# The feed-forward's squared root moved behind the second product, and seven Strassen products on three shared accumulators

## The chip, the cores and the metric

The kernel runs on one core of a Trainium2 chip. The metric is the device time of one execution in microseconds (us): the median of several runs. The profile is a hardware trace of one execution; its span goes from the first instruction to the last.

## What is computed

The reference is a two-layer trunk on one sequence of 512 tokens with 1024 channels. Each layer has an attention part (eight stick-breaking heads and four differential heads) and a feed-forward part; a last RMS norm closes it. The change lies in the feed-forward part and in what follows it:

```python
def rmsnorm(x, g):
    y = xf * lax.rsqrt(jnp.mean(xf * xf, axis=-1, keepdims=True) + EPS) * g
...
    h = rmsnorm(x, mlp_norm[l])
    u = jnp.square(jax.nn.relu(jnp.einsum('bsd,df->bsf', h, w_ff1[l])))   # 1024 -> 4096
    x = x + jnp.einsum('bsf,fd->bsd', u, w_ff2[l])                        # 4096 -> 1024
return rmsnorm(x, final_norm)
```

With r = rsqrt(mean + EPS), one number for each token, the hidden values are relu(r * z)^2 = r^2 * relu(z)^2, since r is positive. So r may be applied before the square, or r^2 = 1 / (mean + EPS) after the second product, where the token lies on the partitions.

## The kernel before

Everything is fp32 carried as two fp32r halves (hi and lo), and each product of two such pairs is three matmuls (`three`, L273: hi by hi, hi by lo, lo by hi). Activations lie transposed, channels on partitions and tokens along the free axis, until the second product of the feed-forward; its result has tokens on partitions.

**One group of the feed-forward.** The 4096 hidden channels go in four groups (`GROUPS`). In a group, eight blocks (`block`, L286) each make 128 hidden channels by 512 tokens in one PSUM bank, 24 matmuls of 512 columns. `evict_u` (L862) takes a block out: relu times r (`rbc`, r spread over the partitions, L872, VectorE), the square (L873, ScalarE), and then the sums and differences of the Winograd form of Strassen's method (tile `F`, one buffer), split into hi and lo (`Ah`, `Al`). The second product is then done as seven products of half size, named in `FORMS`: 11, x3, x2, 22, x1, 21, x4. Each has 24 matmuls too, in two banks (token rows r = 0 and 1), the two rows in turn. `gather` (L891) adds a finished product to its running sum in SBUF, `y[form]`: a ScalarE copy the first time, afterwards a VectorE add (L898).

**Banks.** Of the eight PSUM banks two carry the tag `t` (transposes), two `mm`, three `s`, one `o`. Each of the seven products of the kernel before asks for a fresh pair, (s, s), (s, o) and (mm, mm) in turn, so a pair comes back after two other products.

**The seven sums** are turned into the four quadrants of the result only after the last group: `join` (VectorE, L904) and `merge` (an accumulating transfer from SBUF to SBUF issued by GpSimd, L907).

**The start of a feed-forward.** `rms_a` (L253) turns the squares' sum with four small PE transposes into one column for each row block and takes the power -0.5 on GpSimd. `rms_b` (L267) spreads it with four more transposes and a ScalarE copy into `rbc`. The first two blocks of the first group wait with their eviction until `rbc` is there.

**The ends.** After the first layer `back` (L924) turns the result's columns with four transposes each and adds them to x; four columns run beside the last product x4, the four others beside the first product of the next layer. In the last layer `forth` (L910) turns x into the sums at the start, and the last product x4 is done row 0 first, then row 1 in two column halves (`tail`). While it runs, VectorE and ScalarE finish the other rows: `square` (sum of squares), `root` (VectorE sum, L961, then a power on GpSimd, L963), `weigh` and `store`. `last_row` and `store_last` close the last row. The order of these steps on VectorE is written out in the list `first`, that on ScalarE in `squares`, and `in_order` fixes both.

**Order elsewhere.** A list scheduler places each engine's instructions; program order is its priority, so a step can be put ahead of one that it judges not ready. `behind` fixes single orders. Weight units are split into hi and lo (`split_part`, L110: ScalarE L123 by way of L108, VectorE L124) three units ahead of their use, and the operands of the seven forms grow in place by accumulating transfers (`fetch`, `grow`).

Of the kernel before, what the change touches and what calls it, by code (L numbers as in the profile page):

```python
# [17 lines left out]
P = 128  # L18
# [25 lines left out]
CAME = (4, 5, 6, 7, 0, 1, 2, 3)  # L44
# [117 lines left out]
def trunk(ctx, tc, opened, xT, w, w2, gfin, lamv, cos, sin, out):  # L162
# [62 lines left out]
    ms = cp.tile([P, 4], F32, tag="ms", name="ms")  # L225
    fin = cp.tile([P, 24], F32, tag="fin", name="fin")
    cp.tile([P, 40], F32, tag="trail", name="trail")
# [38 lines left out]

    def rms_b(bc, name, col, tag="t"):  # L267
        pt = bank(tag, "rb_" + name)
        for j in range(4):
            nc.tensor.transpose(pt[:, j * P : (j + 1) * P], col[:, j : j + 1].to_broadcast([P, P]), ident)  # L270
        nc.scalar.copy(bc, pt)

    def three(pt, a, b, first, last):  # L273
        ah, al = a
        bh, bl = b
        nc.tensor.matmul(pt, ah, bh, start=first, stop=False)  # L276
        nc.tensor.matmul(pt, ah, bl, start=False, stop=False)  # L277
        nc.tensor.matmul(pt, al, bh, start=False, stop=last)  # L278
# [33 lines left out]
    for l in range(L):  # L312
        with ExitStack() as actx:
# [52 lines left out]
            came = CAME if l else range(KC)  # L366
# [7 lines left out]
            squares = [add_sq(c, n == 0, tt, nc.vector) for n, c in enumerate(came)]  # L374
# [441 lines left out]
        with ExitStack() as fctx:  # L816
# [4 lines left out]
            y = {f: (fe if f in ("11", "x3") else fp).tile([P, 2, 512], F32, tag="y" + f, name=f"y{f}_{l}") for f in FORMS}  # L821
# [26 lines left out]
            for g in range(GROUPS):  # L848
                for c in range(GP // 2):
                    for form, fn, args in (  # L850
                            ("11", grow, (g, "x1", "12", c)), ("x3", grow, (g, "x2", "11", c)),
                            ("x2", grow, (g, "x4", "21", c)), ("22", grow, (g, "21", "21", c)),
                            ("x1", fetch, (g + 1, "11", c)), ("x4", fetch, (g + 1, "x3", c)),
                            ("21", fetch, (g + 1, "22", c))):
                        if g + 1 < GROUPS or fn is grow:
                            W.then.setdefault(unit(g, form, c), []).append(lambda fn=fn, args=args: fn(*args))
            for form in ("11", "x3", "22"):
                for c in range(GP // 2):
                    fetch(0, form, c)
            W.pools.append(f2)  # L860

            def evict_u(pt, g, k, forms):  # L862
# [9 lines left out]
                nc.vector.scalar_tensor_tensor(out=t, in0=pt, scalar=0.0, in1=rbc, op0=ALU.max, op1=ALU.mult)  # L872
# [12 lines left out]
            fresh = set(FORMS) - ({"21", "22", "x1", "x4"} if last else set())  # L885
            home = {(1, 0): "21", (1, 1): "22", (0, 0): "x4", (0, 1): "x1"}

            def place(tb, j):
                return y[home[(tb // 2, j)]][:, tb % 2, :]

            def gather(form, banks_, rs=(0, 1)):  # L891
                steps = []
                for r in rs:
                    o = y[form][:, r, :]
                    if form in fresh:
                        steps.append(nc.scalar.copy(o, banks_[r]))
                    else:
                        steps.append(nc.vector.tensor_add(o, o, banks_[r]))  # L898
                if 1 in rs:
                    fresh.discard(form)  # L900
                return steps

            def join(to, by):
                return nc.vector.tensor_add(y[to], y[to], y[by])  # L904

            def merge(to, by):
                nc.gpsimd.dma_start(  # L907
                    y[to].rearrange("p a t -> p (a t)"), y[by].rearrange("p a t -> p (a t)"), accum_op=ALU.add)

            def forth(tb, j):  # L910
# [3 lines left out]
                if j == 0:  # L914
                    nc.scalar.copy(place(tb, j), pt)
                elif tb < 2:
                    nc.scalar.activation(y["x1"][:, tb, :], pt, AF.Copy, scale=-1.0)
                else:
                    nc.vector.scalar_tensor_tensor(
                        out=place(tb, j), in0=pt, scalar=-1.0, in1=y["x1"][:, tb - 2, :], op0=ALU.mult, op1=ALU.subtract)  # L920
# [15 lines left out]
            def last_row(banks_):  # L936
                half = [place(1, 0)[:, 0:256], banks_[1][:, 0:256]]
                m = [fin[:, n : n + 1] for n in (8, 9, 10, 11, 0)]
                add = nc.vector.tensor_add(half[0], half[0], banks_[0][:, 0:256])
                ends = [nc.scalar.activation(  # L940
                    ft(f"junk1{n}")[:, 0:256], half[n], AF.Square, accum_out=m[0] if n == 0 else m[4]) for n in range(2)]
# [6 lines left out]
            def store_last(bank_):  # L948
                o, r = place(1, 0), fin[:, 11:12]
                done = store(1, 1, True)  # L950
                for n in range(2):
                    cols = slice(256 * n, 256 * n + 256)
                    nc.vector.scalar_tensor_tensor(
                        out=o[:, cols], in0=bank_[:, 0:256] if n else o[:, cols], scalar=r, in1=cos_t[:, cols],
                        op0=ALU.mult, op1=ALU.mult)
                    nc.sync.dma_start(out[1, :, cols], o[:, cols])
# [13 lines left out]
            def store(tb, j, weighed):  # L970
# [7 lines left out]
                (nc.scalar if (tb, j) == (1, 1) else nc.sync).dma_start(out[tb, :, 512 * j : 512 * j + 512], o)  # L978
# [16 lines left out]
            for g in range(GROUPS):  # L995
                forms = {}
                end = g == GROUPS - 1
                if g == 1:
# [9 lines left out]
                waiting = []  # L1008
                for k in range(2 * GP):
                    for n, pt in enumerate(block(f"f{l}_{g}_{k}", "any")):  # L1010
                        if (g, k, n) == (0, 1, 0):
                            rms_a(ssq, 1.0 / D, rcol, f"m{l}")
                        if (g, k, n) == (0, 2, 4):
                            rms_b(rbc, f"m{l}", rcol)
                    waiting.append((pt, k))
                    if g == 0 and k < 2:
                        continue
                    for one, i in waiting:
                        evict_u(one, g, i, forms)
                    waiting = []  # L1020
# [3 lines left out]
                for f, form in enumerate(FORMS):  # L1024
                    to = [bank((("s", "s"), ("s", "o"), ("mm", "mm"))[f % 3][r], f"{form}{l}{g}{r}") for r in range(2)]
                    work = [(c, i, r, 0) for c in range(GP // 2) for i in range(2) for r in range(2)]
                    tail = end and form == "x4"
                    if tail and last:
                        work = [(c, i, r, n) for r, n in ((0, 0), (1, 1), (1, 2)) for c in range(GP // 2) for i in range(2)]
# [3 lines left out]
                        seed = nc.scalar.copy(halves[1][:, 0:256], y["x4"][:, 1, 256:512])  # L1033
                    elif end and last and form == "21":
                        work.sort(key=lambda e: e[2])
                    held = {}
                    for n, (c, i, r, part) in enumerate(work):
# [10 lines left out]
                        three(pt, (hi[:, SIDE[form], rs], lo[:, SIDE[form], rs]), b_, n == mine[0] and part < 2, n == mine[-1])  # L1048
                        if tail and last and n == 3:
                            squares.append(square(2, 0))  # L1050
# [5 lines left out]
                        if end and not last and form == "x4" and n % 2:  # L1056
                            h = back(4 + n // 2)
# [4 lines left out]
                    came = gather(form, to)  # L1062
                    if not end:
                        continue
                    if form == "11":
                        for to_ in ("x2", "21"):
                            (join if last else merge)(to_, "11")
                    elif form == "x2":
                        merge("x3", "x2")
                        merge("x4", "x3")  # L1070
                        if last:
                            join("22", "x2")
                    elif form == "22" and not last:
                        join("22", "x2")
                    elif form == "x1":
                        if last:
                            join("22", "x1")
                            merge("x1", "x3")
                            squares = [square(tb, 1) for tb in (2, 3)]
                        else:  # L1080
                            in_order(join("22", "x1"), join("x1", "x3"))
            if last:
                add, ends, part, whole = last_row(halves)
                in_order(*first, add, weigh(1, 1), part, store(0, 0, False), whole)
                in_order(*squares, *ends, store(0, 1, True), store_last(halves[1]))
            else:
                W.pools.pop()
                behind(W.rest_of[W.used + 1], columns[4])
                behind(rests[0], columns[5])
                us = [W.next("x", i == 1) for i in range(2)]  # L1090
                pts = [bank("mm", f"p{l + 1}{i}") for i in range(2)]
                gather("x4", to)
                for n, c in enumerate(CAME):
                    if n in (3, 5):
                        for c_ in (n - 3, n - 2):
                            h = back(c_)
                    for i in range(2):
                        three(pts[i], wpair(us[i], c), hpair(c), n == 0, c == CAME[-1])
# [69 lines left out]
```

## Time and profile before

| | |
|---|---|
| median of 3 runs | 1146.51 us (1146.13 to 1146.66) |
| span of the profiled execution | 1144.5 us |
| what lies around the span (each run less that span) | 1.6 to 2.2 us |
| mean granted TensorE clock | 0.999 |
| PE busy | 1137.0 us (99%), 5757 matmuls |
| VectorE (DVE) busy | 843.3 us (74%), 1370 instructions |
| ScalarE (ACT) busy | 611.0 us (53%), 1094 instructions |
| GpSimd (POOL) busy | 149.6 us (13%), 234 instructions |

The profiled execution's own time beyond its span is not listed, so the runs' times stand in for it. Rows of a timeline give the start, the duration, the engine, the line, the operation, what is written and read, and how often in a row. A matmul of 512 columns is shown as 0.39 us long, but one starts every 0.227 us.

### The profile page before, as it was taken

How to read it: one execution, taken by the hardware profiler on the slowest of the kernel's cores; microseconds unless marked ns; L12 is line 12 of the kernel's file. 1: busy time of each engine (PE TensorE's matmuls, PEld its weight loads, DVE VectorE, ACT ScalarE, POOL GpSimd, SP SyncE). 2: the span in 40 equal slices, each digit the busy share in tenths (PEclk: the TensorE clock that was granted, in tenths of full speed). 3: DMA queues.
4: the chain of work that ended last, by engine and by line, in shares of the span. 5: the costliest groups of instructions: out<-in, count | busy, mean ns of one | idle time of the engine just before them, and what ended most of it. 6: DMA issues, size and time to landing. Idle time of an engine off the chain costs nothing.

```text
span 1144.5 us, 15842 instructions
## 1 busy us (share of the span) xinstructions
PE 1137.0 (99%) x5757; PEld 966.4 (84%) x5757; DVE 843.3 (74%) x1370; ACT 611.0 (53%) x1094; POOL 149.6 (13%) x234
## 2 busy tenths in 40 slices
PE   9999999999999999999999999999999999999997
PEld 7899889888888888888888998988888888888886
DVE  7898788767656757757878977887676577576677
ACT  6456666545745444445445666665555354453455
POOL 1000333110101001002000013330110011010011
PEclk9999999999999999999999999999999999999999
DMA  7664353256754755845626634512757647558266
GB/s 251 157 200 140 101 167 103 64 200 159 198 172 95 200 164 92 216 151 95 163 74 186 189 123 135 161 60 80 236 123 198 170 92 200 162 88 230 75 101 175
DMA packets 56860, 170.13 MB, mean 149 GB/s; under 512 B 6992, under 2 KB 8272, under 8 KB 56784
## 3 DMA queue, kind: packets, MB, share of 16 engines
q1 hardware_dynamic: 46128, 131.36, 35.9%
q0 software_dynamic: 10224, 37.23, 19.0%
q8 instruction: 45, 0.74, 0.3%
q10 hardware_dynamic: 432, 0.56, 0.1%
q14 instruction: 31, 0.25, 0.1%
HBM read 138.18 MB, written 2.10 MB: 123 GB/s over the span
## 4 chain that ended last, share of the span: by engine, by line
PE 98%; DVE 0%; issue 0%; DMA 0%; POOL 0%; ACT 0%; POOLq 0%; DVEq 0%; SPq 0%; ACTq 0%
PE f L276 10%; PE f L278 10%; PE f L277 10%; PE x L276 5%; PE x L277 5%; PE x L278 5%; PE wo L276 3%; PE wo L277 3%; PE wo L278 3%; PE T1s L596 1%; PE T0s L596 1%; PE p1w L418 1%; PE p0w L418 1%; PE p0w L419 1%; PE p1w L419 1%; PE p0u L419 1%
## 5 line engine op out<-in xcount | busy, mean ns | idle before, releaser
L108 ACT ACTIVATE whi<-raw 128x1024 fp32r<-128x1024 f32 (+1 forms) x130 | 131.8, 1018 | 139.9 <-PE f L277 43.0
L276 PE MATMUL f<-h_hi,whi 128*128 128x512 f32 x512 | 199.9, 390 | 0.0
L278 PE MATMUL f<-h_hi,wlo 128*128 128x512 f32 x512 | 199.3, 389 | 0.0
L277 PE MATMUL f<-h_lo,whi 128*128 128x512 f32 x512 | 199.2, 389 | 0.0
L124 DVE TENSOR_TENSOR wlo<-raw,whi 128x1024 fp32r<-128x1024 f32 (+1 forms) x130 | 154.0, 1189 | 54.4 <-ACT whi L108 52.7
L108 ACT ACTIVATE whi<-q 128x512 fp32r<-128x512 f32 x224 | 128.1, 623 | 109.5 <-PE x L278 46.1
L124 DVE TENSOR_TENSOR wlo<-q,whi 128x512 fp32r<-128x512 f32 x224 | 145.1, 686 | 34.5 <-ACT whi L108 34.3
L278 PEld LDWEIGHTS f<-h_hi,wlo 128*128 128x128 f32 x512 | 96.1, 188 | 20.1
L277 PEld LDWEIGHTS f<-h_lo,whi 128*128 128x128 f32 x512 | 96.1, 188 | 19.7
L276 PEld LDWEIGHTS f<-h_hi,whi 128*128 128x128 f32 x512 | 96.1, 188 | 19.7
L231 DVE TENSOR_TENSOR Al<-F,Ah 128x256 fp32r<-128x256 f32 (+2 forms) x96 | 74.7, 778 | 45.2 <-ACT Ah L230 45.2
L276 PE MATMUL x<-whi,Ah 128*128 128x512 f32 (+1 forms) x256 | 99.5, 389 | 0.0
L278 PE MATMUL x<-whi,Al 128*128 128x512 f32 (+1 forms) x256 | 99.2, 388 | 0.0
L277 PE MATMUL x<-wlo,Ah 128*128 128x512 f32 (+1 forms) x256 | 99.2, 387 | 0.0
L230 ACT ACTIVATE Ah<-F 128x256 fp32r<-128x256 f32 (+2 forms) x96 | 67.5, 703 | 57.1 <-DVE F L881 55.1
L845 POOL DMA_DIRECT2D q<-in_w x48 | 42.5, 885 | 393.3 <-DVE wlo L124 360.5
L872 DVE SCALAR_TENSOR_TENSOR F<-f,rbc 128x512 f32<-128x512 f32 x64 | 43.6, 688 | 67.8 <-PE f L278 55.6
L873 ACT ACTIVATE F<-F 128x512 f32<-128x512 f32 x64 | 39.9, 624 | 39.0 <-DVE F L872 38.9
L278 PEld LDWEIGHTS x<-whi,Al 128*128 128x128 f32 x256 | 48.1, 188 | 9.9
L276 PEld LDWEIGHTS x<-whi,Ah 128*128 128x128 f32 x256 | 48.1, 188 | 9.7
L277 PEld LDWEIGHTS x<-wlo,Ah 128*128 128x128 f32 x256 | 48.1, 188 | 9.7
L235 ACT ACTIVATE h_hi<-x,begin 128x512 fp32r<-128x512 f32 x32 | 22.7, 721 | 30.2 <-DVE x L735 19.4
(987 smaller groups left out, 2609.1 us busy)
## 6 DMA issues: line engine op xcount, KB each, us to landing
raw<-in_w SPq DMA_DIRECT2D x126, 512.0 KB, 3.7
q<-in_w SPq DMA_DIRECT2D x64, 512.0 KB, 4.9
q<-in_w POOLq DMA_DIRECT2D x64, 512.0 KB, 5.6
yx<-yx POOLq DMA_DIRECT2D x5, 512.0 KB, 4.4
x<-in_xT SPq DMA_DIRECT2D x8, 256.0 KB, 4.3
out_xT<-y SPq DMA_DIRECT2D x4, 256.0 KB, 2.0
raw<-in_w SPq DMA_DIRECT2D x6, 128.0 KB, 4.1
cos_t<-in_cos SPq DMA_DIRECT2D x2, 256.0 KB, 5.1
```

The source lines that it names most:

```text
L108: return self.nc.scalar.activation(o, src, AF.Copy)
L124: self.last = h, nc.vector.tensor_tensor(out=lo[:, a:b], in0=raw[:, a:b], in1=hi[:, a:b].bitcast(F32), op=ALU.subtract)
L230: a = nc.scalar.activation(hi, src, AF.Copy)
L231: nc.vector.tensor_tensor(out=lo, in0=src, in1=hi.bitcast(F32), op=ALU.subtract)
L276: nc.tensor.matmul(pt, ah, bh, start=first, stop=False)
L277: nc.tensor.matmul(pt, ah, bl, start=False, stop=False)
L278: nc.tensor.matmul(pt, al, bh, start=False, stop=last)
L418: nc.tensor.matmul(o, h_hi[:, c, t], wl, start=False, stop=False)
L419: W.product = nc.tensor.matmul(o, h_lo[:, c, t], wh, start=False, stop=c == KC - 1 and q == 1)
L845: nc.gpsimd.dma_start(t, quad(g, q, c), accum_op=ALU.add)
L872: nc.vector.scalar_tensor_tensor(out=t, in0=pt, scalar=0.0, in1=rbc, op0=ALU.max, op1=ALU.mult)
L873: nc.scalar.activation(t, t, AF.Square)
```

## The change

The factor r^2 is applied where a sum leaves PSUM. `rms_square` takes the place of `rms_a` and `rms_b` at the head of the feed-forward; it has the four transposes of `rms_a`, a mean and a reciprocal. `evict_u` is a ScalarE relu and the same square. The seven products come in the order 11, x3, x2, 21, x1, x4, 22 and run on three pairs of banks held for the whole second product of a group: X (11, then x2, x1 and 22 added on top), V (x3, then x4 on top), Y (21). After each product its pair, as it then stands, is scaled by r^2 and added to one of four sums, the quadrants themselves. The joins and merges are gone. In the last group of the last layer X is also taken into the fourth quadrant before the last product 22, which then runs on fresh banks.

```diff
-FORMS = ("11", "x3", "x2", "22", "x1", "21", "x4")
+FORMS = ("11", "x3", "x2", "21", "x1", "x4", "22")
+CHAIN = {"11": "X", "x2": "X", "x1": "X", "22": "X", "x3": "V", "x4": "V", "21": "Y"}
+SUMS = {"11": (1, 0), "x3": (0, 1), "x2": (0, 0), "21": (1, 0), "x1": (0, 1), "x4": (0, 0), "22": (1, 1)}
...
+    def rms_square(src, name):
+        pt = bank("t", "rs_" + name)
+        for j in range(4):
+            nc.tensor.transpose(pt[:, j * P : (j + 1) * P], src[:, j * P : (j + 1) * P], ident)
+        nc.vector.tensor_reduce(out=mean, in_=pt.rearrange("p (j f) -> p j f", j=4), axis=AX.X, op=ALU.add)
+        nc.vector.tensor_scalar(out=mean, in0=mean, scalar1=1.0 / D, scalar2=EPS, op0=ALU.mult, op1=ALU.add)
+        nc.vector.reciprocal(r2, mean)
...
-                nc.vector.scalar_tensor_tensor(out=t, in0=pt, scalar=0.0, in1=rbc, op0=ALU.max, op1=ALU.mult)
+                nc.scalar.activation(t, pt, AF.Relu)
                 nc.scalar.activation(t, t, AF.Square)
...
+            def gather(quad, banks_, rs=(0, 1)):
+                for r in rs:
+                    tb = 2 * quad[0] + r
+                    o, by = place(tb, quad[1]), r2[:, tb : tb + 1]
+                    if quad in fresh:
+                        steps.append(nc.scalar.activation(o, banks_[r], AF.Copy, scale=by))
+                    else:
+                        steps.append(nc.vector.scalar_tensor_tensor(
+                            out=o, in0=banks_[r], scalar=by, in1=o, op0=ALU.mult, op1=ALU.add))
...
-            def join(to, by):
-            def merge(to, by):
...
+                turn[0] = 0
...
                         if (g, k, n) == (0, 1, 0):
-                            rms_a(ssq, 1.0 / D, rcol, f"m{l}")
-                        if (g, k, n) == (0, 2, 4):
-                            rms_b(rbc, f"m{l}", rcol)
-                    waiting.append((pt, k))
-                    if g == 0 and k < 2:
-                        continue
+                            rms_square(ssq, f"m{l}")
+                    evict_u(pt, g, k, forms)
...
-                    to = [bank((("s", "s"), ("s", "o"), ("mm", "mm"))[f % 3][r], f"{form}{l}{g}{r}") for r in range(2)]
+                chains = {n: [bank(t, f"{n}{l}{g}{r}") for r, t in enumerate(tags)]
+                          for n, tags in (("X", "ss"), ("Y", "so"), ("V", ("mm", "mm")))}
+                    opens = form in ("11", "x3", "21")
...
                         if tail and last and n == 3:
-                            first = [came[0], weigh(2, 1), root(2), weigh(3, 1), came[1]]
-                            squares += [seed, square(3, 0), store(2, 1, True), square(0, 1), square(1, 1)]
-                            first += [store(2, 0, False), root(3), store(3, 0, False), *gather("x4", to, (0,))]
-                            squares += [square(0, 0), store(3, 1, True)]
-                            first += [weigh(0, 1), root(0)]
+                            squares.append(square(0, 0))
+                            first += [root(0), store(0, 0, False), came[1]]
+                            squares += [seed, store(0, 1, True), square(1, 0)]
+                            first += [root(1), store(1, 0, False), *gather(total, to, (0,))]
+                            squares += [store(1, 1, True), square(2, 1)]
+                            first.append(root(2))
...
+                    if end and last and form == "x1":
+                        done = ((2, 0), (3, 0), (0, 1), (1, 1))
+                        squares = [square(*e) for e in done]
+                        weighed = [weigh(*e) for e in done]
+                    elif end and last and form == "x4":
+                        first = [came[0]]
             if last:
                 add, ends, part, whole = last_row(halves)
-                in_order(*first, add, weigh(1, 1), part, store(0, 0, False), whole)
-                in_order(*squares, *ends, store(0, 1, True), store_last(halves[1]))
+                in_order(*first, add, part, store(2, 1, False), whole)
+                in_order(*squares, *ends, store(2, 0, True), store_last(halves[1]))
```

Other edits follow from these: `back` turns the columns 0 to 3 first, all of `forth` is on ScalarE, the operands of the forms are fetched in the new order, and the last row's second half is stored with gains that already hold r^2.

More of the change, by code (lines that the diff above doesn't have):

```diff
@@ L365, in trunk @@
                     m[:, 2 * i : 2 * i + 2, :].rearrange("p e t -> p (e t)") for m in (md_hi, md_lo))
-            came = CAME if l else range(KC)
             if l:
@@ L373, in trunk @@
                 behind(W.last[1], opened[1])
-            squares = [add_sq(c, n == 0, tt, nc.vector) for n, c in enumerate(came)]
+            squares = [add_sq(c, c == 0, tt, nc.vector) for c in range(KC)]
             behind(squares[0][0], opened[0])
@@ L948, in store_last @@
             def store_last(bank_):
-                o, r = place(1, 0), fin[:, 11:12]
-                done = store(1, 1, True)
+                o = place(3, 1)
+                done = store(3, 0, True)
                 for n in range(2):
@@ L1032, in trunk @@
                             halves[1][:, 0:256], zeros[:, 0:128], zeros[:, 128:384], start=True, stop=False)
-                        seed = nc.scalar.copy(halves[1][:, 0:256], y["x4"][:, 1, 256:512])
-                    elif end and last and form == "21":
+                        seed = nc.scalar.activation(
+                            halves[1][:, 0:256], place(3, 1)[:, 256:512], AF.Copy, scale=mean[:, 3:4])
+                    elif end and last and form == "x4":
                         work.sort(key=lambda e: e[2])
@@ L1061, in trunk @@
                         break
[L1062 to L1081, printed above, removed]
+                    came = gather(total, to)
```

98 lines of the change are left out of this document (45 added, 53 removed).

## The prediction, made before the changed kernel ran

> **What bounds the kernel now.** I read the page first, then the PE's waits, then the chain of waits, then the groups of instructions, and last the timeline at three places: a turn from one product to the next, the end of layer 0, the tail.
>
> ```profile
> span 1144.5 us, 15842 instructions
> PE 1137.0 (99%) x5757; PEld 966.4 (84%) x5757; DVE 843.3 (74%) x1370; ACT 611.0 (53%) x1094; POOL 149.6 (13%) x234
> PE 98%; DVE 0%; issue 0%; DMA 0%; POOL 0%; ACT 0%; POOLq 0%; DVEq 0%; SPq 0%; ACTq 0%
> PE warm L216 <- POOL edge L210: 1.4, 1, 1.4
> PE S0d L509 <- DMA kl0d0k<-hl0d0k: 0.2, 1, 0.2
> ```
>
> The first three lines are the page's: span, busy times, and the share of each engine in the chain that ended last. The last two are the whole answer of the PE's waits: 1.4 us before the first matmul and 0.2 us in layer 0's attention. So PE is bound by its own matmuls from start to tail, and in the feed-forward it waits for nothing. Three things can move the time: PE work taken away, a new PE wait, or the tail behind the last matmul. Work moved between VectorE and ScalarE counts only through these.
>
> **PE work.** The change keeps every matmul. It drops the four transposes of the spread root, once a layer. In the chain of waits they are
>
> ```profile
> 255.81 0.44 PE rb_m L270 x4
> 822.07 0.44 PE rb_m L270 x4
> ```
>
> so 2 x 0.44 = 0.88 us less, all on the path: 1144.5 - 0.9. The four transposes of the sum of squares stay. Its reciprocal on four columns, in no row here, lies beside the second block; r^2 is first read after product 11, some 45 us later (eight blocks and one product of 24 matmuls each, one every 0.226 us, as the turn below shows). Cost zero; if that cover were gone, a fraction of a microsecond once a layer.
>
> **VectorE and ScalarE.** The groups:
>
> ```profile
> L872 DVE SCALAR_TENSOR_TENSOR F<-f,rbc 128x512 f32<-128x512 f32 x64 | 43.6, 688 | 67.8 <-PE f L278 55.6
> L873 ACT ACTIVATE F<-F 128x512 f32<-128x512 f32 x64 | 39.9, 624 | 39.0 <-DVE F L872 38.9
> L898 DVE TENSOR_TENSOR yx<-yx,x 128x512 f32<-128x512 f32 x51 | 33.5, 683 | 3.7 <-DMA yx<-y 2.9
> L896 ACT COPY yx<-x 128x512 f32<-128x512 f32 x12 | 6.9, 587 | 4.1 <-PE x L278 3.6
> L904 DVE TENSOR_TENSOR y<-y,yx 128x1024 f32<-128x1024 f32 x4 | 4.9, 1218 | 0.0
> ```
>
> and two rows of the tail's timeline, for a column as factor and for the rounding of a weight unit's two halves:
>
> ```profile
> 1133.49 0.75 DVE L976 SCALAR_TENSOR_TENSOR y<-y,fin,cos_t 128x512 f32<-128x512 f32 x1
> 1127.44 1.15 ACT L108 ACTIVATE whi<-q 128x512 fp32r<-128x512 f32 x2 [1.57 <-PE x L278]
> ```
>
> VectorE loses 64 relus (43.6 us) and the seven joins (7 x 1.22 = 8.5 us). A product is still gathered after each of the seven: "four sums" saves space and joins, not gathers. But only the first visit to each of layer 0's four sums is a ScalarE copy now (by the code 8 copies for 20; the row shows those of one name), and the last group takes X out once more, so VectorE gets 14 more gathers, at 0.683 (as before) to 0.75 (a column as factor): +10 us. VectorE falls by about 42 us to 801 (70%). ScalarE gets 64 relus out of PSUM, no row of before; by the nearest rows, 587 ns (a copy out of PSUM) to 624 ns (the square in SBUF), I take 600: +38, less 12 copies (7): about 642 (56%). Neither is near PE's 99%, so none of it moves the time by itself. The five accumulating transfers of the merges go as well; nobody on the path waits for them.
>
> **The shared accumulators** add a wait: x2 may not add to X before 11 is read out, x1 not before x2, 22 not before x1, x4 not before x3. Queued behind a waiting matmul are all later ones. One product lies between, where two lay before. The tightest place in the last group:
>
> ```profile
> 1105.26 0.39 PE L278 MATMUL 11131_10338<-whi,Al 128*128 128x512 f32 x1
> 1105.00 0.69 DVE L898 TENSOR_TENSOR y<-y,11130_10337 128x512 f32<-128x512 f32 x1 [0.87 <-PE 11130_10337 L278]
> 1105.61 1.22 DVE L231 TENSOR_TENSOR Al<-F,Ah 128x1024 fp32r<-128x1024 f32 x1
> 1106.74 1.29 DVE L124 TENSOR_TENSOR wlo<-q,whi 128x512 fp32r<-128x512 f32 x2
> 1107.95 0.68 DVE L898 TENSOR_TENSOR y<-y,11131_10338 128x512 f32<-128x512 f32 x1
> 1110.92 0.39 PE L276 MATMUL x<-whi,Ah 128*128 128x512 f32 x1
> ```
>
> The last matmul of 11 starts at 1105.26, x2 begins 25 matmuls on at 1110.92 (0.226 us each), its row 1 three more on (1111.60). Row 0 is gathered at once, row 1 only by 1108.63, behind a split of forms and two of weights. Slack 2.97 us. In the changed kernel VectorE has one relu less just there, but the forms follow a relu on ScalarE that may stand behind a weight unit's rounding (1.15), so I expect 1.8 to 3 us left. Cost: zero.
>
> **The end of layer 0.** The first transposes beside the last product read now what x4 has only just left; before, that sum was a product older.
>
> ```profile
> 561.35 1.22 DVE L904 TENSOR_TENSOR yx<-yx,yx 128x1024 f32<-128x1024 f32 x1
> 562.48 1.22 DVE L124 TENSOR_TENSOR wlo<-raw,whi 128x1024 fp32r<-128x1024 f32 x1
> 563.62 0.68 DVE L898 TENSOR_TENSOR y<-y,21030_5273 128x512 f32<-128x512 f32 x1
> 564.22 0.68 DVE L898 TENSOR_TENSOR y<-y,21031_5274 128x512 f32<-128x512 f32 x1
> 564.15 0.38 PE L927 MATMUL yT<-edge,yx 128*128 128x128 f32 x2
> ```
>
> With these times the gathers end at 564.90 and the transposes, due at about 564.0, would wait 0.9 us, or about 1.1 with the longer gathers. But the join at 561.35 (1.22) goes, so weight half and gathers move up and end at about 563.8. I take zero; ends 0 and +1.1.
>
> **The tail.** Its order is new, so I walk it in the old clock.
>
> ```profile
> 1129.74 0.39 PE L278 MATMUL 21130_10552<-whi,Al 128*128 128x512 f32 x1
> 1130.45 0.68 DVE L898 TENSOR_TENSOR y<-y,21130_10552 128x512 f32<-128x512 f32 x1
> 1131.21 0.61 ACT L933 ACTIVATE spare<-y 128x512 f32<-128x512 f32 x1
> 1131.95 0.21 DVE L961 TENSOR_SCALAR fin<-fin 128x1 f32<-128x1 f32 x1 [0.22 <-ACT spare L933]
> 1132.25 0.95 POOL L963 TENSOR_TENSOR fin<-fin,mhalf 128x1 f32<-128x1 f32 x1 [0.97 <-DVE fin L961]
> 1132.88 0.69 DVE L898 TENSOR_TENSOR y<-y,21131_10553 128x512 f32<-128x512 f32 x1
> 1133.61 0.63 ACT L933 ACTIVATE spare<-y 128x512 f32<-128x512 f32 x1 [0.22 <-DVE y L898]
> 1134.65 0.55 POOL L963 TENSOR_TENSOR fin<-fin,mhalf 128x1 f32<-128x1 f32 x1 [1.45 <-DVE fin L961]
> 1135.32 0.39 PE L278 MATMUL x<-whi,Al 128*128 128x512 f32 x1
> 1135.91 0.68 DVE L898 TENSOR_TENSOR yx<-yx,x 128x512 f32<-128x512 f32 x1
> 1137.57 0.41 DVE L939 TENSOR_TENSOR yx<-yx,x 128x256 f32<-128x256 f32 x1
> 1138.30 0.28 PE L278 MATMUL half<-whi,Al 128*128 128x256 f32 x1
> 1138.76 0.74 DVE L976 SCALAR_TENSOR_TENSOR yx<-yx,fin,cos_t 128x512 f32<-128x512 f32 x1
> 1139.42 0.15 DVE L944 TENSOR_TENSOR fin<-fin 128x1 f32<-128x1 f32 x1
> ```
>
> The last product's row 0 ends at 1135.71 and is gathered 0.2 later (1135.91); from there a serial chain runs to the last sum at 1139.42, only a quarter microsecond behind what the last matmul allows. Any lateness of that gather goes to the end. Before, VectorE took the next-to-last product's row 1 (1132.88) ahead of the first store. The new list has row 0, root, store, row 1, root, store, and then this gather, and each store waits for square, root and power. From one gather to the gather behind the next store: gather to square 0.73 (1132.88 to 1133.61), square to root 0.74, root to power 0.30, power 0.55, store 0.7 (0.75 long, less the overlap of two in a row): 3.0 to 3.1. From 1130.40 the critical gather stands at 1130.40 + 2 x 3.05 = 1136.5, and at 1136.9 if the first power takes 0.95 as here. Against 1135.91 that is +0.6 to +1.0; I take +0.75. Two things widen it. The four weighings and the two extra gathers of X are outside the written order; if VectorE does them ahead of the first gather it starts up to 1.6 later: +2.5. If instead the store leaves more room than I count, the weighing that is gone between the two last sums can win back 0.25: -0.25.
>
> **Sum.** -0.9 (transposes) + 0.75 (tail) + 0 (products, layer end) = -0.15 on 1144.5; carried to the median, 1146.51 - 0.2 = **1146.3 us**.
>
> **The rivals.** *A wait takes the place of none (slower).* The gather in a chain comes too late. It decides from 2.97 us of extra lateness on; one form split (1.22), two weight halves (1.29) and one rounding on ScalarE (1.15) in front of it make 3.7, so 0.7 us of PE wait. In every group, that is 8 x 0.7 = 5.6, and 1146.3 + 5.6 = 1151.9 us. For it: row 1 is gathered almost three microseconds after row 0 already. Against it: the relus leave VectorE. Chance 0.19. The Trainium skill, Perfetto Trace Analysis, section Matmuls, speaks against this change: independent matmul groups should rotate through different PSUM banks, so that one's evacuation overlaps the next one's matmuls. By that rule at its worst, nothing overlapped, the change's 31 returns to a pair (four a group, one less in the last) would each show two gathers, some 42 us in all, an estimate from the gather's row. The trace bears out only the weaker form: in the new order a full product, 5.4 us, still lies between two uses of a pair.
>
> *The tail goes long* (+2.5): 1146.5 - 0.9 + 2.5 = 1148.1. Chance 0.17.
>
> *The tail holds* (between -0.25 and +0.2): 1145.4 to 1145.8. For it: a different placing of the loose steps. Chance 0.16.
>
> *The change does not do what it says*, in that it still gathers seven times a group; that is built into my sum. *A large gain*: it needs 2.3 us and I find no PE wait that could give it; 0.05 for what I don't see. The forecast keeps 0.43.
>
> **How the numbers follow.** 0.2% is 2.3 us, about what a measurement of this kernel can tell from no change. Forecast and holding tail lie within it, the long tail mostly (with the layer's end at +1.1 it leaves: 0.04). Same 0.43 + 0.16 + 0.13 = 0.72; slower 0.19 + 0.04 = 0.23; faster 0.05. The range goes from 1146.13 - 0.9 - 0.25, rounded to 1145.0, to 1146.51 - 0.9 + 2.5 + 1.1 = 1149.2; outside lie most of the accumulators' rival and of the large gain.
>
> **What would show it.** PE has 5749 matmuls, no row of the spread root in a feed-forward, and the same two waits. VectorE near 801 us, ScalarE near 642. The first transposes at layer 0's end follow x4's second gather within 0.2 us. In the tail the last product's row 0 is gathered about 0.8 us (not 0.2) after its last matmul's end, and everything behind it moves along. I am wrong if the PE's waits name a gather, or if the span after the last matmul is shorter than now.

## The result: 1157.4 us, 1% slower

| | before | after |
|---|---|---|
| median of 4 runs each, same chip | 1146.59 us (1146.13 to 1148.11) | 1157.43 us (1157.35 to 1158.41) |
| ratio after / before | | 1.0096 [1.0082, 1.0110] |
| span of the profiled execution | 1144.5 us | 1156.5 us |

The forecast was 1146.3 us, at most 1149.2. The page of the changed kernel, span, busy times and the chain that ended last:

```profile
span 1156.5 us, 15843 instructions
PE 1146.8 (99%) x5749; PEld 964.4 (83%) x5749; DVE 811.3 (70%) x1313; ACT 642.3 (56%) x1147; POOL 141.2 (12%) x225
PE 96%; DVE 1%; DMA 1%; ACT 1%; issue 1%; POOL 0%; POOLq 0%; DVEq 0%; ACTq 0%
```

and the whole answer of its PE's waits:

```profile
PE warm L217 <- POOL edge L211: 1.4, 1, 1.4
PE S0s L519 <- DMA kl0s1k<-hl0s1q: 0.5, 1, 0.5
```

There are eight matmuls fewer, as the change says, and yet PE is busy for 9.8 us more. It waits 1.9 us in all, for 1.6 before, all of it ahead of the first feed-forward. So the time didn't come in as a wait: the matmuls themselves became slower. Which ones, the groups of instructions say. First two rows of the kernel before, the feed-forward's blocks `f` and the seven second products; then the same lines of the kernel after (L276 has become L287):

```profile
L276 PE MATMUL f<-h_hi,whi 128*128 128x512 f32 x512 | 199.9, 390 | 0.0
L276 PE MATMUL x<-whi,Ah 128*128 128x512 f32 (+1 forms) x256 | 99.5, 389 | 0.0
```

```profile
L287 PE MATMUL f<-h_hi,whi 128*128 128x512 f32 x512 | 202.9, 396 | 0.0
L287 PE MATMUL X<-whi,Ah 128*128 128x512 f32 x248 | 96.9, 391 | 0.0
```

The blocks `f` went from a mean of 390 to 396 ns; the second product, the part that the change rewrites, stands at 391 against 389 (the row of its X alone; by their starts, X steps 227.0 ns and V and Y 226.7, for 226.8 before). The blocks are code that the change does not touch. A timeline of a few of their matmuls, before and after, shows it as a step from one start to the next:

```profile
339.75 0.39 PE L276 MATMUL f<-h_hi,whi 128*128 128x512 f32 x1
340.43 0.39 PE L276 MATMUL f<-h_hi,whi 128*128 128x512 f32 x1
341.11 0.39 PE L276 MATMUL f<-h_hi,whi 128*128 128x512 f32 x1
```

```profile
339.70 0.40 PE L287 MATMUL f<-h_hi,whi 128*128 128x512 f32 x1
340.40 0.40 PE L287 MATMUL f<-h_hi,whi 128*128 128x512 f32 x1
341.10 0.40 PE L287 MATMUL f<-h_hi,whi 128*128 128x512 f32 x1
```

Two other matmuls lie between the rows shown, so six steps took 1.36 us before and 1.40 after. Over all 1536 matmuls of the blocks, from the differences of their starts in the traces (steps with a gap left out), the mean step is 226.8 ns before and 233.3 after: 1536 x 6.5 ns = 10.0 us.

The 12.0 us of span (1144.52 to 1156.48), by the times at which the stages start in the two traces:

| stretch | after less before |
|---|---|
| to the first block of layer 0's feed-forward | +0.8 us |
| 32 blocks and 3 groups of second products, layer 0 | +4.7 us |
| from there to the first block of layer 1's feed-forward | +0.3 us |
| the same blocks and products, layer 1 | +4.5 us |
| the last group's seven second products | 0.0 us |
| from the last matmul's start to the end | +1.7 us |

The 9.2 us of the two feed-forwards are 10.0 of slower blocks less 0.9 for the transposes of the spread root. The tail gave 1.7. The 0.8 us ahead of the first block are scatter: that stretch ends between 240.2 and 242.1 us in the twelve traces of this case, fast blocks or slow. The stretch between the layers (+0.3 us) is 277.2 to 277.6 us long in the seven traces with fast blocks and 277.5 to 278.3 in the five with slow ones. The projections of the attention part are the likely cause; they read `h` and weights as the blocks do and step longer too: those of the differential heads 228.3 to 228.5 ns on the mean in the seven traces and 232.1 to 233.2 in the five (steps with a gap left out). How much of the 0.3 us is theirs doesn't show against that scatter.

### The profile page after: what moved, and what is told of

It is laid out like the page before. It is cut to its first block, busy times and chain, and to the rows that moved or that the text cites. A ratio compares the mean times of both kernels' runs of the same rounds, so it can differ in the third digit from the quotient of the medians.

```text
span 1156.5 us, 15843 instructions
## 1 busy us (share of the span) xinstructions
PE 1146.8 (99%) x5749; PEld 964.4 (83%) x5749; DVE 811.3 (70%) x1313; ACT 642.3 (56%) x1147; POOL 141.2 (12%) x225
## 4 chain that ended last, share of the span: by engine, by line
PE 96%; DVE 1%; DMA 1%; ACT 1%; issue 1%; POOL 0%; POOLq 0%; DVEq 0%; ACTq 0%
PE f L287 10%; PE f L288 10%; PE f L289 10%; PE X L287 5%; PE X L288 5%; PE X L289 5%; PE wo L287 3%; PE wo L288 3%; PE wo L289 3%; PE V L287 2%; PE V L289 2%; PE V L288 2%; PE Y L287 1%; PE Y L289 1%; PE Y L288 1%; PE T1s L606 1%
## 5 line engine op out<-in xcount | busy, mean ns | idle before, releaser
L287 PE MATMUL f<-h_hi,whi 128*128 128x512 f32 x512 | 202.9, 396 | 0.0
L288 PE MATMUL f<-h_lo,whi 128*128 128x512 f32 x512 | 202.5, 395 | 0.0
L287 PEld LDWEIGHTS f<-h_hi,whi 128*128 128x128 f32 x512 | 96.2, 188 | 23.0
L287 PE MATMUL X<-whi,Ah 128*128 128x512 f32 x248 | 96.9, 391 | 0.0
L288 PE MATMUL X<-wlo,Ah 128*128 128x512 f32 x248 | 96.6, 389 | 0.0
L289 PE MATMUL X<-whi,Al 128*128 128x512 f32 x248 | 96.5, 389 | 0.0
L289 PEld LDWEIGHTS X<-whi,Al 128*128 128x128 f32 x248 | 46.5, 188 | 9.8
L287 PEld LDWEIGHTS X<-whi,Ah 128*128 128x128 f32 x248 | 46.6, 188 | 9.6
L288 PEld LDWEIGHTS X<-wlo,Ah 128*128 128x128 f32 x248 | 46.5, 188 | 9.6
L287 PE MATMUL V<-whi,Ah 128*128 128x512 f32 x128 | 49.8, 389 | 0.0
L288 PE MATMUL V<-wlo,Ah 128*128 128x512 f32 x128 | 49.8, 389 | 0.0
L289 PE MATMUL V<-whi,Al 128*128 128x512 f32 x128 | 49.8, 389 | 0.0
```

Source lines behind the costliest of these rows:

```text
L287: nc.tensor.matmul(pt, ah, bh, start=first, stop=False, skip_group_check=goes_on)
L288: nc.tensor.matmul(pt, ah, bl, start=False, stop=False, skip_group_check=goes_on)
L289: nc.tensor.matmul(pt, al, bh, start=False, stop=last, skip_group_check=goes_on)
```

## The experiments

### What else changed: the place of the tiles

The cut diff above leaves out these lines:

```diff
+    mean = cp.tile([P, 4], F32, tag="mean", name="mean")
+    r2 = cp.tile([P, 4], F32, tag="r2", name="r2")
     fin = cp.tile([P, 24], F32, tag="fin", name="fin")
-    cp.tile([P, 40], F32, tag="trail", name="trail")
+    cp.tile([P, 32], F32, tag="trail", name="trail")
```

`trail` is never read nor written. It only fills space between the small tiles and everything that is allocated behind them: the weight units, the forms, the sums. A second such tile, `lead`, stands in front of the activations `h`. Two new tiles of 16 bytes for each partition were paid for with 32 bytes less of `trail`. But in the compiled program each of the two takes 32 bytes (`mean` at 62720, `r2` at 62752, `fin` at 62784), so everything behind stands 32 bytes further: the first weight unit at 75296 instead of 75264, with `h_hi` at 19456 as before. Before, both were multiples of 256.

*Theory A:* a matmul of a block is slower because its two operands, `h` and the weights, no longer stand at the same place within 256 bytes. *Rival B:* the change itself does it, by the ScalarE relu reading PSUM beside the matmuls or by accumulators held over several products. *Rival C:* it is the place of the weights alone, whatever `h` does.

The first three kernels. The changed kernel, with the two tiles paid for in full:

```diff
-    cp.tile([P, 32], F32, tag="trail", name="trail")
+    cp.tile([P, 24], F32, tag="trail", name="trail")
```

> The changed kernel with the filler tile at the end of the constants 24 columns wide, not 32. Theory A (addresses): the two new columns of four floats, mean and r2, take 64 bytes of each partition, the filler gave back only 32, so every weight tile starts 32 bytes past a multiple of 64 while h_hi and h_lo start on one, and a matmul that reads both steps every 233 ns, not 227. With 24 columns the weights stand at their old addresses: the feed-forward blocks step at 227 again, the time falls by 10 to 11 us to about 1146.9, and only the later tail (+1.7) less the dropped transposes (-0.9) stands against the kernel before. Theory B (the relu on ScalarE reads PSUM beside the matmuls and slows them): nothing changes, 1157.4. Theory C (waits on the shared banks): nothing changes either.

The kernel before, with nothing of the change but the filler's size, so that its weights stand 32 bytes nearer:

```diff
-    cp.tile([P, 40], F32, tag="trail", name="trail")
+    cp.tile([P, 32], F32, tag="trail", name="trail")
```

> The kernel before, with its own filler tile cut from 40 to 32 columns, nothing else: weights at 32 past a multiple of 64. Theory A: its feed-forward blocks step at 233 ns, +10.1 us there and 0.5 to 1 in the attention's projections, so about 1157. Theories B and C: 1146.5, as before.

The changed kernel 32 bytes further on, and so 64 off:

```diff
-    cp.tile([P, 32], F32, tag="trail", name="trail")
+    cp.tile([P, 40], F32, tag="trail", name="trail")
```

> The changed kernel with a filler of 40 columns: weights at a multiple of 64 but not of 128. Theory A with a line of 64 bytes: as fast as with 24 columns, about 1146.9. Theory A with 128 bytes: still about 1157. Theories B and C: 1157.4.

The changed kernel with the smaller filler took 1146.81 us, 1.0004 [0.9995, 1.0013] of the kernel before: the loss is gone with eight columns of a tile that nothing uses. The kernel before with the smaller filler took 1158.37 us, 1.0103 [1.0088, 1.0119], with no other edit. The third took 1157.87, 1.0101 [1.0084, 1.0118]. Busy times and the blocks' row on the page of the changed kernel with 24:

```profile
PE 1136.6 (99%) x5749; PEld 965.8 (84%) x5749; DVE 811.3 (71%) x1313; ACT 641.2 (56%) x1147; POOL 140.9 (12%) x225
L287 PE MATMUL f<-h_hi,whi 128*128 128x512 f32 x512 | 199.7, 390 | 0.0
```

and on that of the kernel before with 32:

```profile
PE 1148.6 (99%) x5757; PEld 965.0 (83%) x5757; DVE 844.0 (73%) x1370; ACT 611.7 (53%) x1094; POOL 149.7 (13%) x234
L276 PE MATMUL f<-h_hi,whi 128*128 128x512 f32 x512 | 202.9, 396 | 0.0
L276 PE MATMUL x<-whi,Ah 128*128 128x512 f32 (+1 forms) x256 | 99.5, 389 | 0.0
```

With the old 1370 VectorE instructions and the old order of products the blocks cost 396 ns; with the new ones they cost 390. That ends rival B. The last row is a control inside the same run: in the second product both operands, weights and forms, lie behind the filler and moved together, and it stays at 389.

### Weights alone, or the distance

The next four move `h` too, or choose other distances. `lead` larger by 32 bytes, so that `h` and the weights both move on by 32 and stay 32 apart:

```diff
-    cp.tile([P, 32], F32, tag="lead", name="lead")
+    cp.tile([P, 40], F32, tag="lead", name="lead")
```

> The changed kernel with the filler at the start of the constants 40 columns wide, not 32: now h_hi and h_lo (the moving operand of the feed-forward blocks) start 32 past a multiple of 64, the weights (the stationary one) on a multiple. If what counts is that the two operands differ by 32: blocks step at 233 ns as in the changed kernel, and the second product, whose operands all lie among the weights, stays at 227: about 1157. If only the stationary operand's address counts: 227 everywhere, about 1146.9. If the moving operand's counts as well: slower than 233.

That edit together with the `trail` of 24, so that neither stands on a multiple of 256 but both 32 behind one:

```diff
-    cp.tile([P, 32], F32, tag="lead", name="lead")
+    cp.tile([P, 40], F32, tag="lead", name="lead")
...
-    cp.tile([P, 32], F32, tag="trail", name="trail")
+    cp.tile([P, 24], F32, tag="trail", name="trail")
```

> Filler at the start 40 wide, filler at the end 24: both h_hi and h_lo and all weights start 32 past a multiple of 256. If the matmul slows down when its two operands differ in their place within a line: 227 ns everywhere, about 1146.9 us. If the weights have to start on a multiple of 128 or 256 by themselves: the feed-forward blocks step at 233 ns, about 1157.

A `trail` of 56, for a distance of 128:

```diff
-    cp.tile([P, 32], F32, tag="trail", name="trail")
+    cp.tile([P, 56], F32, tag="trail", name="trail")
```

> Filler at the end 56 wide: the weights start 128 past a multiple of 256, h_hi and h_lo on a multiple; the distances 32, 64 and 224 were slow. If the line is 128 bytes: 227 ns, about 1146.9. If it is longer: 233 ns, about 1157.

And one of 88, for a distance of 256:

```diff
-    cp.tile([P, 32], F32, tag="trail", name="trail")
+    cp.tile([P, 88], F32, tag="trail", name="trail")
```

> Filler at the end 88 wide: the weights start 256 bytes later than in the kernel before, so the distance to h_hi is an odd multiple of 256 where it was a multiple of 512. Distances of 32, 64, 128 and -32 from that were slow. If the line is 256 bytes: 227 ns, about 1146.9 us. If it is 512 or more: about 233 ns and 1157.

All of them in one table. The places are bytes in a partition, from the compiled programs; the step is the mean over the blocks, from the starts in each trace; each ratio is to runs of the kernel before on the same chip.

| kernel | `h_hi` | `whi` | distance modulo 256 | step of `f` | ratio to before |
|---|---|---|---|---|---|
| before | 19456 | 75264 | 0 | 226.8 ns | 1 |
| after | 19456 | 75296 | 32 | 233.3 ns | 1.0096 [1.0082, 1.0110] |
| after, trail 24 | 19456 | 75264 | 0 | 226.8 ns | 1.0004 [0.9995, 1.0013] |
| before, trail 32 | 19456 | 75232 | 224 | 233.3 ns | 1.0103 [1.0088, 1.0119] |
| after, trail 40 | 19456 | 75328 | 64 | 233.3 ns | 1.0101 [1.0084, 1.0118] |
| after, lead 40 | 19488 | 75328 | 32 | 233.3 ns | 1.0094 [1.0079, 1.0109] |
| after, lead 40, trail 24 | 19488 | 75296 | 0 | 226.8 ns | 1.0006 [0.9996, 1.0016] |
| after, trail 56 | 19456 | 75392 | 128 | 233.1 ns | 1.0108 [1.0089, 1.0126] |
| after, trail 88 | 19456 | 75520 | 0 | 226.8 ns | 1.0006 [0.9996, 1.0016] |

The weights at 75296 are slow beside an `h` at 19456 and fast beside one at 19488. So it isn't their place (rival C) but how the two stand to each other, and the one shift by 256 that was tried is fast again. The mean step has two levels and no slope: 32 costs as much as 128 (the single steps differ: mostly 231, 232 and 235 ns at 32, and 229, 230, 237 and 238 at 128). The blocks' rows on the pages of the two kernels with the larger `lead`, without and with the smaller `trail`:

```profile
L287 PE MATMUL f<-h_hi,whi 128*128 128x512 f32 x512 | 202.9, 396 | 0.0
L287 PE MATMUL X<-whi,Ah 128*128 128x512 f32 x248 | 96.9, 391 | 0.0
```

```profile
L287 PE MATMUL f<-h_hi,whi 128*128 128x512 f32 x512 | 199.7, 390 | 0.0
```

The filler moves the tiles of other engines as well: most of what VectorE and ScalarE read and write beside the blocks also lies behind it. That their work slows the matmuls is a rival that no edit here tests, but the traces speak against it. Take only the block steps with no instruction on VectorE, ScalarE or GpSimd from 0.23 us ahead of the matmul's start to 0.46 us behind it: the changed kernel has 189 of them, mean 233.5 ns, and the kernel before 128, mean 226.7. Eleven of the 189 have no DMA packet beside them either; their mean is 233.1. The longer step comes without that work.

Theory A holds for every distance that was tried. Other distances, and ones below 32, were not. What in the chip reads more slowly stays open too: the traces show the longer step, and nothing that PE waits for.

### The tail

The changed kernel with a `trail` of 24 has the change and no misplaced tile, so its tail can be read in the old clock (its last matmul starts at 1138.19, before at 1138.30). VectorE in its timeline:

```profile
1130.49 0.75 DVE L909 SCALAR_TENSOR_TENSOR y<-V,r,y 128x512 f32<-128x512 f32 x1
1131.15 1.40 DVE L909 SCALAR_TENSOR_TENSOR y<-X,r,y 128x512 f32<-128x512 f32 x2
1132.47 0.21 DVE L963 TENSOR_SCALAR fin<-fin 128x1 f32<-128x1 f32 x1
1133.37 0.75 DVE L978 SCALAR_TENSOR_TENSOR y<-y,fin,cos_t 128x512 f32<-128x512 f32 x1 [0.69 <-POOL fin L965]
1134.04 0.74 DVE L909 SCALAR_TENSOR_TENSOR y<-V,r,y 128x512 f32<-128x512 f32 x1
1136.52 0.75 DVE L978 SCALAR_TENSOR_TENSOR y<-y,fin,cos_t 128x512 f32<-128x512 f32 x1 [0.67 <-POOL fin L965]
1137.18 0.74 DVE L909 SCALAR_TENSOR_TENSOR y<-Z,r,y 128x512 f32<-128x512 f32 x1
1140.81 0.15 DVE L946 TENSOR_TENSOR fin<-fin 128x1 f32<-128x1 f32 x1
```

The critical gather, y<-Z, starts at 1137.18, 1.97 us behind the start of its last matmul:

```profile
1135.21 0.39 PE L289 MATMUL Z<-whi,Al 128*128 128x512 f32 x1
```

Before it was 0.59 (1135.32 to 1135.91). Both stores in front of it wait for GpSimd's power (0.69 and 0.67), and the gathers behind each can only follow. So two stores were put behind the gathers that they kept back, each gather ahead of its store:

```diff
-                            first += [root(0), store(0, 0, False), came[1]]
+                            first += [root(0), came[1], store(0, 0, False)]
...
-                            first += [root(1), store(1, 0, False), *gather(total, to, (0,))]
+                            first += [root(1), *gather(total, to, (0,)), store(1, 0, False)]
```

(with the `trail` of 24, as in the two kernels that follow)

> Filler 24 wide, and in the written order of the tail each gather of a finished row goes ahead of the store that stood before it. Theory (the last product's row 0 is gathered 2.0 us, not 0.6, after its last matmul because two stores stand in front of it, each waiting for square, root and power): that gather comes within 0.8 us, the tail is 1.2 to 1.5 us shorter, about 1145.5. Rival (the tail is long because VectorE has too much to do before the first of these gathers, the four weighings and the two extra gathers of X): at most 0.3 us shorter, about 1146.6.

It took 1145.31 us beside 1146.31, ratio 0.9993 [0.9984, 1.0002]. VectorE in its tail:

```profile
1132.77 0.75 DVE L909 SCALAR_TENSOR_TENSOR y<-V,r,y 128x512 f32<-128x512 f32 x1
1133.43 0.74 DVE L978 SCALAR_TENSOR_TENSOR y<-y,fin,cos_t 128x512 f32<-128x512 f32 x1
1135.63 0.75 DVE L909 SCALAR_TENSOR_TENSOR y<-Z,r,y 128x512 f32<-128x512 f32 x1 [0.70 <-PE Z L289]
1139.26 0.15 DVE L946 TENSOR_TENSOR fin<-fin 128x1 f32<-128x1 f32 x1
```

Now VectorE waits at the critical gather for PE (0.70 <-PE Z), where PE's sum had waited for VectorE, and the last sum stands at 1139.26 instead of 1140.81. From the last matmul's start to the end it is 6.19 us, against 7.73 in the kernel without the edit and 6.22 before. That is the tail's 1.5 us, found and given back. The four weighings and the two extra gathers, the rival's cause, were still there. This version is faster than the changed kernel by all of its 1%, and its ratio is the lowest of the runs; against the kernel before its interval still holds 1.

A further reordering also put the two extra gathers of X into the written order and the last sum ahead of the store beside it:

```diff
-                        gather(total, to)
+                        extra = gather(total, to)
...
-                            first += [root(0), store(0, 0, False), came[1]]
+                            first += [extra[0], root(0), extra[1], came[1], store(0, 0, False)]
...
-                in_order(*first, add, part, store(2, 1, False), whole)
+                in_order(*first, add, part, whole, store(2, 1, False))
```

(and the critical gather ahead of its store, as above)

> As the one before, with the two extra gathers of X put around the first root, and the last sum ahead of the last store of row 2. Theory: the stores are the whole of the delay, so this adds 0.1 to 0.4 us of gain by taking the last sum from behind a store: about 1145.2, faster than the kernel before by the transposes' 0.9 us and a little. Rival: VectorE's load is the cause, then the two extra gathers, moved apart, bring 0.4 or nothing: 1146.2 to 1146.8.

It took 1145.93, 0.9997 [0.9988, 1.0006], and its tail is longer by 0.4 us (6.58) where 0.1 to 0.4 less was expected; the rival's 1146.2 to 1146.8 didn't come either. VectorE and GpSimd in its last microseconds:

```profile
1138.49 0.16 DVE L946 TENSOR_TENSOR fin<-fin 128x1 f32<-128x1 f32 x1 [0.47 <-ACT spare L941]
1138.57 0.74 DVE L978 SCALAR_TENSOR_TENSOR y<-y,fin,sin_t 128x512 f32<-128x512 f32 x1
1138.73 0.98 POOL L947 TENSOR_TENSOR fin<-fin,mhalf 128x1 f32<-128x1 f32 x1 [1.33 <-DVE fin L946]
```

The last power takes 0.98 us, where the same step in the kernel just before has

```profile
1139.49 0.54 POOL L947 TENSOR_TENSOR fin<-fin,mhalf 128x1 f32<-128x1 f32 x1 [1.43 <-DVE fin L946]
```

The store that was put behind the last sum now runs while GpSimd takes the last power. Counted from the last matmul's start the sum came 0.11 us earlier (0.97 for 1.08) and the power took 0.44 longer: the order that looked better on VectorE's own list cost more on GpSimd's. That rests on one trace of each.

### The relu's engine

Rival B once more, for the part of the change that moves 64 relus: the changed kernel with the `trail` of 24, and the relu back on VectorE.

```diff
-                nc.scalar.activation(t, pt, AF.Relu)
+                nc.vector.tensor_scalar(out=t, in0=pt, scalar1=0.0, scalar2=1.0, op0=ALU.max, op1=ALU.mult)
```

> Filler 24 wide, and the relu of the feed-forward's eviction put back on VectorE (a maximum with zero, the root still behind the second product). Theory: no PE wait hangs on which engine does the relu, so the time is that of the changed kernel with a filler of 24, 1146.8 within 0.5 us; VectorE gains about 44 us of busy time, ScalarE loses about 38. Rival B (ScalarE's reading of PSUM costs the matmuls something): 0.5 us or more faster, and a step below 226.8 ns in the feed-forward blocks.

It took 1147.09 us beside 1146.31, ratio 1.0006 [0.9997, 1.0016]; with the relu on ScalarE it was 1.0004. The blocks' step stays at 226.8 ns. On its page:

```profile
PE 1136.1 (99%) x5749; PEld 966.2 (84%) x5749; DVE 848.7 (74%) x1377; ACT 607.0 (53%) x1083; POOL 141.0 (12%) x225
```

VectorE gained 37 us by it and ScalarE lost 34, less than the 44 and 38 expected, and the time shows none of it: within what these runs can tell apart, the move of work between the two engines is worth nothing here.

## Why the prediction was wrong, step by step

**PE work, the step that failed.** "The change keeps every matmul" was right (5749 of them, as forecast) and the conclusion "so 2 x 0.44 = 0.88 us less" was not. It took the step of 0.226 us over as a constant of the matmul, and its list of what can move the time (PE work taken away, a new PE wait, the tail) had no place for the same matmuls taking longer. The step is one of this placement of operands: 226.8 or 233.3 ns in the blocks, by the distance of `h` and weights. The term is -0.9 + 10.0, and perhaps some tenths for the projections. The four transposes did go: with the old step, the stretch of 32 blocks and three groups of products is 288.59 us for 289.05 in layer 0 and 292.22 for 292.69 in layer 1, some 0.47 each for the forecast 0.44.

The evidence was in the diff: a filler tile whose size changes is an edit of addresses, and the forecast gave it no term, no bound and no rival. The trace of before could not have priced it: all its matmuls of this shape (128x128 by 128x512, fp32r) have their operands at distance 0. But a rival "same instructions, another step" belonged beside the other rivals. That the time came out 10 us off is no luck of a run: five programs with a distance other than 0 show it and none with distance 0 does.

**The shared accumulators: zero, as forecast.** The rival that had the largest chance did not come. In the kernel with the `trail` of 24, the last group's gather of row 1 of 11 and the turn from row 0 to row 1 in x2, from the timeline:

```profile
1107.91 0.75 DVE L909 SCALAR_TENSOR_TENSOR y<-X,r,y 128x512 f32<-128x512 f32 x1
1111.28 0.39 PE L289 MATMUL X<-whi,Al 128*128 128x512 f32 x1
1111.50 0.39 PE L287 MATMUL X<-whi,Ah 128*128 128x512 f32 x1
```

The gather ends at 1108.66. The last two rows are x2's third matmul, the last of its row 0, and its fourth, which opens row 1 at 1111.50: 2.84 us are left, within the 1.8 to 3 of the forecast. PE's waits of the changed kernel name no gather.

**The end of layer 0: zero, as forecast.** In the changed kernel's timeline:

```profile
567.99 1.40 DVE L909 SCALAR_TENSOR_TENSOR y<-V,r,y 128x512 f32<-128x512 f32 x2
569.64 0.60 PE L926 MATMUL yT<-edge,y 128*128 128x128 f32 x4
```

The gathers of x4 end at 569.39, 0.25 us ahead of the first transposes. The forecast was that these follow within 0.2 us, so it named the right neighbours and was 0.05 short; that PE doesn't wait shows in the stretch from the last block to these transposes, 34.230 us before and 34.230 with the `trail` of 24.

**The tail: the mechanism right, the size too small.** The stores do keep the critical gather back, as written. The term was +0.75, ends -0.25 and +2.5; it measured 1.5 (7.73 less 6.22; 7.73 to 7.92 in the eight traces with this written order), inside the ends. The gather was put at 1136.5 to 1136.9 and came at 1137.18, or 1137.28 in the old clock. Three parts were mis-sized: the first gather starts 0.2 later than the walk had it; from a gather to its square it is 0.84, not 0.73, so that a free step is 3.14 (1134.04 to 1137.18); and the first step is 3.55, because the two extra gathers of X (1131.15, 1.40 long) ran between the gather and its root and pushed the root to 1132.47. The forecast knew that these two were loose and thought only of a place ahead of the first gather.

**VectorE and ScalarE.** Forecast 801 and 642 us, measured 811.3 and 642.3. The gathers with a column as factor take 0.74 to 0.75, not 0.683; 0.06 on the 105 of them is some 6 of the 10 us that were missing; the rest was not followed up. It is off the path, as said.

**The sum of the other terms.** With the operands in their old relation the change measured 1146.81 us for a forecast of 1146.3. Its profiled span is 1.4 us longer than before: 1.5 of the tail, less 0.9 of transposes, and 0.8 in the two attention parts, which scatter by as much. Its runs are not to be told from no change. Every term that the forecast costed in time was within its ends; what it did not look at cost 10 us.

## What to carry to other kernels

A tile added or resized moves every tile behind it. When PE is the bound, read the places of both matmul operands out of the compiled program before and after an edit, and compare the step from one matmul's start to the next in code that was not edited: if the busy time of PE changes and its count does not, look there first. And when a list of steps is written out by hand, put what the last product's chain needs ahead of what merely could be done by then.

## What the runs showed of the hardware that was not expected

- **Operands at the same place within 256 bytes.** In the feed-forward's blocks a 512-column fp32r matmul stepped 226.8 ns with stationary and moving operand at the same place modulo 256 bytes of their partitions (also when both stood 32 off, and when the weights were shifted by 256), and 233.1 to 233.3 at differences of 32, 64, 128 and 224: up to 2.9% more. Distance 0 alone doesn't give the short step: the projections of the stick-breaking heads, which other matmuls break up, have it too and step 230.9 ns on the mean before (232.2 after). Why was not followed up.
- **GpSimd beside VectorE.** A power of one column took 0.54 to 0.57 us in most of the tails. It took 0.98 where it began 0.16 us after a VectorE product of operands in SBUF (above), and 0.95 in the kernel before, where its row at 1132.25 (quoted in the prediction) begins within

```profile
1132.09 0.68 DVE L968 TENSOR_TENSOR y<-y,sin_t 128x512 f32<-128x512 f32 x1
```

  (0.95 again in the kernel before with a `trail` of 32). Where the power began first, it stayed short although such a product ran through most of it; in the kernel before:

```profile
1137.74 0.54 POOL L963 TENSOR_TENSOR fin<-fin,mhalf 128x1 f32<-128x1 f32 x1 [2.53 <-DVE fin L961]
1137.90 0.69 DVE L968 TENSOR_TENSOR yx<-yx,sin_t 128x512 f32<-128x512 f32 x1
```

  Where the VectorE operation that was running read PSUM, as a gather of X did in the second reordering, it stayed at 0.57. That is a handful of cases and no experiment of its own.
